# 512 weight columns to a bank per token tile in three projections of a two-layer backbone

## The chip, the cores and the metric

The kernel runs on one core of one Trainium2 chip. The metric is the time of one execution in microseconds on the device. Before the change, three runs gave a median of 1530.77 us (1530.55 to 1533.98).

## The reference, cut to what matters

The reference is a backbone of two layers over 256 latent tokens and 256 context tokens with 2048 channels, all in float32. An even layer (neighbourhood attention beside an S5 state-space group, one output projection) is followed by an odd layer (grouped-query attention). The three projections that the change touches are these:

```
# layer 0, for x (256 tokens) and for the context (256 tokens)
y = concat([za * silu(g_a), zb * silu(g_b)], -1) @ w_out        # ev_w_out 2048 x 2048
x = layer_norm(DN_ALPHA * x + gt * y, ln_g, ln_b)
# layer 1: w_in = [q 2048 | k 512 | v 512 | g 2048] columns
q, k, v, g = split(h @ w_in);  q, k = rms_norm(q), rms_norm(k)  # od_w_in; k, v for all 512 tokens
o = attention(rope(q), [rope(k), kc], [v, vc])                  # 16 heads over 4 key/value heads
y = (o * silu(g)) @ w_out                                       # od_w_out 2048 x 2048, 256 tokens
out = layer_norm(DN_ALPHA * x + gt * y, ln_g, ln_b)
```

## The kernel before

All work is in tiles of 128 partitions. The activations lie transposed, 16 channel tiles by 512 tokens, as a high part `big_h` and a low part `big_l`, both in the rounded type fp32r. Columns 0 to 255 are the context and 256 to 511 are x, until the last attention writes its output for x into the first 256. A *half* is one of these, two token tiles of 128. A product is made of three matmuls (high by high, high by low, low by high).

The weights come in pieces of 1024 columns by 128 partitions (512 KB) through the class `Stream` (lines 338 to 419). A piece passes through a DMA on SyncE's queue into a `raw` buffer, through ScalarE, which rounds it into a `hi` buffer, and through VectorE, which subtracts the two into a `lo` buffer (called the low part here). `fill` (line 395) issues these three steps ahead of use: low parts up to as many pieces ahead as there are `lo` buffers, high parts up to the number of `hi` buffers. There are 4 raw, 4 hi and 3 lo buffers, one more hi and lo from the output projection of layer 0 on (line 1557), and 3 hi and 4 lo more in the last projection (line 1864). `get` calls `fill` and hands out one piece. Each engine runs its instructions in the order in which the program issues them.

In the three projections a piece is 4 channel tiles by 256 weight columns, and `bform` and `bpart` (lines 497 and 506) put a block of 256 columns for both token tiles into one PSUM bank: per piece 2 token tiles by 4 channel tiles by 3 matmuls of 256 columns, 24 in all, and 4 pieces to a block. Two banks (`mm`, line 265) are used in turn. Five further banks (`bb2`, line 1554) serve transposes and attention.

- Output projection of layer 0 (`layer0_half`, line 1578): 8 blocks for the context half, then 8 for the x half. The first two blocks are begun ahead of the attention part's last writes (lines 1545 to 1549). After each block VectorE multiplies by the gate, adds the scaled input and takes the statistics (lines 1593 to 1596); this is called the eviction. The gate row is loaded by a DMA on SyncE's queue (line 1570).
- Between this and the next stage the x half is normalised in the background (`norm_h1`, line 1599), and tables for the rotary positions are made on VectorE from two small rows `grows` that come by DMA (lines 1658 to 1668).
- Keys and values (lines 1718 to 1730): for each half 2 blocks of keys and 2 of values. A block of keys goes through `k_done` (line 1695): ScalarE copies and squares, VectorE sums, GpSimd makes the inverse root, VectorE scales, TensorE transposes.
- Queries, gates and attention (lines 1800 to 1819) are not touched, but they share the banks.
- Output projection of layer 1 (lines 1820 to 1897): 2 blocks begun beside the last attention pair, 4 more, and a last part that does the last two blocks for the first token tile, then for the second, so that the first tile can be normalised while the second is still multiplied.

Background work (generators) is put between matmuls by `pump`, by due times that a model of the engines inside the program gives (class `Clock`). The model prices a 512-column matmul at 0.2162 and a 256-column one at 0.1082 (line 227).

Of the kernel before, what the change touches and what calls it, by code (L numbers as in the profile page):

```python
# [30 lines left out]
P = 128  # L31
D = 2048
# [216 lines left out]
def backbone(ctx: ExitStack, tc: tile.TileContext, A, out):  # L249
# [15 lines left out]
    mm = pool(ctx, name="mm", bufs=2, space=bass.MemoryType.PSUM)  # L265
# [26 lines left out]
    def mbank():  # L292
        return mm.tile([P, 512], F32, name="m")
# [44 lines left out]
    class Stream:  # L338
# [181 lines left out]

    def bform4(done):
# [60 lines left out]
    for half in range(2):  # L582
        for n in range(0, 8, 2):
            for n_, ko in ((0, 1), (1, 1), (0, 0), (1, 0)) if n == 0 and half == 0 else ((0, 1), (0, 0), (1, 1), (1, 0)):
                ws.add(W_OUT, D, ko * 8, 8, (n + n_) * 256, 256)
    for half in range(2):
        for n in range(4):
            for ko in (0, 1):
                ws.add(X_IN, OD_IN, ko * 8, 8, 2048 + n * 256, 256)
# [5 lines left out]
    NX = 2  # L595
    for n, a in ([(n, a) for n in range(NX) for a in range(3)] + [(n, 3) for n in range(NX)]
                 + [(n, a) for n in range(NX, 8) for a in range(4)]):
        ws.add(X_OUT, D, a * 4, 4, n * 256, 256)
# [946 lines left out]
    ps0 = [mbank().rearrange("p (t n) -> p t n", t=2) for _ in range(2)]  # L1545
    for i in range(4):
        if i == 1:
            zab = background(za_split())
        bpart(ps0[i // 2], 0, OUT_ORDER, i % 2)
# [4 lines left out]
    bb = pool(ctx, name="bb2", bufs=5, space=bass.MemoryType.PSUM)  # L1554
# [23 lines left out]
    def layer0_half(hf):  # L1578
# [3 lines left out]
        st_ = tp.tile([P, 2, 8, 6], F32, name="st0", bufs=2)  # L1582
        for n in range(8):
            cs = slice(n * 256, n * 256 + 256)
            xp = op.tile([P, 2, 256], F32, name="xp", bufs=2)
            GP.dma_start(xp, dram(src, n * 256, [[D, P], [P * D, 2], [1, 256]]))
            if hf == 0 and n < 2:
                ps = ps0[n]
                for a in (2, 3):
                    bpart(ps, 0, OUT_ORDER, a)  # L1590
            else:
                ps = bform(hf * T, OUT_ORDER)
            V.tensor_mul(t[:, :, cs], ps, gate[:, v, None, cs].to_broadcast([P, 2, 256]))
            V.scalar_tensor_tensor(t[:, :, cs], xp, ALPHA, t[:, :, cs], op0=OP.mult, op1=OP.add)
            for i in range(2):
                V.bn_stats(st_[:, i, n], t[:, i, cs])
# [75 lines left out]
    def rms(ps4):  # L1672

        sq = w1.tile([P, 2, 2, P], F32, name="sq", bufs=1).rearrange("p a b d -> p (a b) d")
        act(sq, ps4, AF.Square)
        ss = w1.tile([P, 4], F32, name="ss")
        V.tensor_reduce(ss, sq, axis=AX.X, op=OP.add)
# [17 lines left out]
    def k_done(hf, n, ps):  # L1695
        kn = w1.tile([P, 4, P], F32, name="kn")
        act(kn, ps.rearrange("p t (h d) -> p (t h) d", h=2))
        r = rms(kn)
        yield
        V.tensor_mul(kn, kn, r[:, :, None].to_broadcast([P, 4, P]))  # L1700
        kf = w1.tile([P, 2, 2, P], F32, name="kf")
        if hf == 0:
            V.tensor_mul(kf.rearrange("p t h d -> p (t h) d"), kn, grows[:, 1, None, :].to_broadcast([P, 4, P]))
        else:
            rope(kf, kn.rearrange("p (t h) d -> p t h d", t=2), 1)
        yield
        p = bank()
        for h in range(2):
            for t_ in range(2):
                PE.transpose(p[:, h * T + t_ * P:h * T + (t_ + 1) * P], kf[:, t_, h], ident)  # L1710
        o = slice(hf * T, hf * T + T)
# [248 lines left out]
```

## Time and profile before

| | |
|---|---|
| median of three runs | 1530.77 us |
| the profiled execution, its own time | 1534.4 us |
| its span, first to last instruction | 1532.5 us |
| TensorE matmuls (PE) busy | 1478.4 us, 96% |
| VectorE (DVE), ScalarE (ACT), GpSimd (POOL) busy | 982.8, 641.7, 154.1 us |
| mean granted TensorE clock | 0.986 |
| chain that ended last | PE 79%, DVE 7%, DMA 7%, issue 4% |

PE is busy in nearly every slice of the span, but a busy PE also holds what each matmul costs beside its columns. The chain is followed back from the last instruction to what released it at each step. The output projection of layer 0 lies between about 867 and 1073 us of the span, keys and values up to 1166 us, the attention stage up to 1441 us and the last projection up to 1517 us.

### The profile page before, as it was taken

How to read it: one execution, taken by the hardware profiler on the slowest of the kernel's cores; microseconds unless marked ns; L12 is line 12 of the kernel's file. 1: busy time of each engine (PE TensorE's matmuls, PEld its weight loads, DVE VectorE, ACT ScalarE, POOL GpSimd, SP SyncE). 2: the span in 40 equal slices, each digit the busy share in tenths (PEclk: the TensorE clock that was granted, in tenths of full speed). 3: DMA queues.
4: the chain of work that ended last, by engine and by line, in shares of the span. 5: the costliest groups of instructions: out<-in, count | busy, mean ns of one | idle time of the engine just before them, and what ended most of it. 6: DMA issues, size and time to landing. Idle time of an engine off the chain costs nothing.

```text
span 1532.5 us, 30530 instructions
## 1 busy us (share of the span) xinstructions
PE 1478.4 (96%) x12530; PEld 1283.4 (84%) x12530; DVE 982.8 (64%) x1721; ACT 641.7 (42%) x981; POOL 154.1 (10%) x308
## 2 busy tenths in 40 slices
PE   6998988999999999999999999999999999999996
PEld 3676777667789977888878999999899999999995
DVE  5356479988622688554447765665666666677597
ACT  2332244422355443433335533443454565665540
POOL 1000000000000033300000000100421211121021
PEclk8999999999999999999999999999999999999998
DMA  9998374676889577658877698886465445444684
GB/s 326 335 330 265 119 220 144 208 248 203 261 286 298 166 201 166 162 192 239 251 215 230 199 348 297 285 300 200 147 223 178 133 149 151 125 124 152 205 259 142
DMA packets 329919, 332.70 MB, mean 217 GB/s; under 512 B 40196, under 2 KB 287924, under 8 KB 329140
## 3 DMA queue, kind: packets, MB, share of 16 engines
q1 hardware_dynamic: 323540, 314.87, 65.8%
q0 software_dynamic: 6240, 15.88, 3.9%
q8 instruction: 98, 1.61, 0.4%
q14 instruction: 41, 0.34, 0.1%
HBM read 301.92 MB, written 24.54 MB: 213 GB/s over the span
## 4 chain that ended last, share of the span: by engine, by line
PE 79%; DVE 7%; DMA 7%; issue 4%; POOL 2%; SPq 1%; ACT 1%; DVEq 0%; POOLq 0%; ACTq 0%
PE m L212 59%; PE b L212 11%; PE a L212 6%; PE sb L212 4%; DVE dd L212 2%; DMA aw<-in_ada_w_dram 2%; DMA raw<-in_ev_w_in_dram 1%; DVE t L212 1%; SPq L212 1%; DVE lo L212 1%; DMA nat<-in_s_c_im_dram 1%; DMA gf<-in_ln_b_dram 1%; POOL gbr L212 1%; POOL rt L212 1%; DMA nat<-in_s_c_re_dram 1%
## 5 line engine op out<-in xcount | busy, mean ns | idle before, releaser
L212 ACT ACTIVATE hi<-raw 128x1024 fp32r<-128x1024 f32 (+1 forms) x253 | 265.2, 1050 | 319.2 <-PE m L212 166.5
L212 PE MATMUL m<-hi,big_h 128*128 128x256 f32 x1224 | 351.8, 287 | 0.1
L212 PE MATMUL m<-hi,big_l 128*128 128x256 f32 x1224 | 347.3, 284 | 0.0
L212 DVE TENSOR_TENSOR lo<-raw,hi 128x1024 fp32r<-128x1024 f32 (+1 forms) x214 | 257.2, 1209 | 110.9 <-issue 55.4
L212 PE MATMUL m<-lo,big_h 128*128 128x256 f32 x1152 | 326.9, 284 | 0.0
L212 PE MATMUL m<-big_h,hi 128*128 128x512 f32 (+1 forms) x848 | 319.6, 377 | 2.1 <-DVE acc L212 1.4
L212 PE MATMUL m<-big_l,hi 128*128 128x512 f32 (+1 forms) x848 | 309.3, 365 | 0.0
L212 PE MATMUL m<-big_h,lo 128*128 128x512 f32 (+1 forms) x832 | 304.6, 366 | 0.0
L212 PEld LDWEIGHTS m<-hi,big_h 128*128 128x128 f32 x1224 | 235.6, 192 | 7.3 <-issue 6.6
L212 PEld LDWEIGHTS m<-hi,big_l 128*128 128x128 f32 x1224 | 235.6, 193 | 0.2 <-DVE big_l L212 0.2
L212 PEld LDWEIGHTS m<-lo,big_h 128*128 128x128 f32 x1152 | 222.0, 193 | 0.1
L212 PEld LDWEIGHTS m<-big_h,hi 128*128 128x128 f32 x848 | 160.2, 189 | 39.9 <-issue 11.7
L212 PEld LDWEIGHTS m<-big_h,lo 128*128 128x128 f32 x832 | 157.1, 189 | 26.4
L212 PEld LDWEIGHTS m<-big_l,hi 128*128 128x128 f32 x848 | 160.5, 189 | 21.2
L212 PE MATMUL m<-lox,big_h 128*128 128x256 f32 x384 | 108.6, 283 | 0.0
L212 PE MATMUL m<-hix,big_h 128*128 128x256 f32 x312 | 89.1, 285 | 0.0
L212 PE MATMUL m<-hix,big_l 128*128 128x256 f32 x312 | 88.3, 283 | 0.0
L212 POOL DMA_DIRECT2D Yd<-ys x64 | 38.0, 600 | 407.7 <-DVE ys L212 407.0
L212 PEld LDWEIGHTS m<-lox,big_h 128*128 128x128 f32 x384 | 73.6, 192 | 0.3
L212 ACT ACTIVATE hix<-raw 128x1024 fp32r<-128x1024 f32 x45 | 47.5, 1056 | 49.9 <-PE m L212 16.9
L212 PE MATMUL a<-aw,cst 128*32 128x256 f32 x1024 | 65.4, 384 | 2.5 <-DMA aw<-in_ada_w_dram 2.4
L212 DVE TENSOR_TENSOR lox<-raw,hi 128x1024 fp32r<-128x1024 f32 x39 | 47.6, 1221 | 21.6 <-PE m L212 14.6
(383 smaller groups left out, 2192.9 us busy)
## 6 DMA issues: line engine op xcount, KB each, us to landing
aw<-in_ada_w_dram SPq DMA_DIRECT2D x128, 512.0 KB, 5.8
raw<-in_od_w_in_dram SPq DMA_DIRECT2D x96, 512.0 KB, 3.8
raw<-in_ev_w_in_dram SPq DMA_DIRECT2D x90, 512.0 KB, 5.0
adp<-in_ada_w_dram SPq DMA_DIRECT2D x64, 512.0 KB, 8.6
raw<-in_ev_w_out_dram SPq DMA_DIRECT2D x64, 512.0 KB, 6.1
raw<-in_od_w_out_dram SPq DMA_DIRECT2D x32, 512.0 KB, 4.9
ub<-Ud SPq DMA_DIRECT2D x32, 128.0 KB, 5.1
Sd<-sx SPq DMA_DIRECT2D x16, 256.0 KB, 6.5
```

The costliest lines, as they stand in the source:

```text
L212: r = f(*a, **kw)
```

## The change

In the three projections a piece becomes 2 channel tiles by 512 weight columns, and a PSUM bank holds 512 columns of one token tile. `wide` replaces `bform` there: a block of 512 columns takes two banks, one for each token tile, and 8 pieces, two at a time. With two pieces at hand it does both for the first token tile, then both for the second (24 matmuls of 512 columns in all). With the last two pieces (`a == 6`) no low parts are issued ahead before the first tile's bank is evicted (`done(0)`); then the low parts of two pieces (`ws.fill(2)`), then the second tile's matmuls and its eviction. The low and high parts of the next block's later pieces are issued as before, up to the number of buffers ahead, each time two pieces are taken.

The two `mm` banks become a ring of two single banks, to which a third is added from the output projection of layer 0 on; `bb2` has 4 banks in place of 5. The eviction is done for one token tile and 512 columns where it was two token tiles and 256. Keys: one token tile and four heads, where it was two token tiles and two heads. The last projection: three blocks of 512 columns (the first begun beside the last attention pair with 6 of its 8 pieces), and a last part of 512 columns for the first token tile and twice 256 for the second.

```diff
-    mm = pool(ctx, name="mm", bufs=2, space=bass.MemoryType.PSUM)
+    mm = pool(ctx, name="mm", bufs=1, space=bass.MemoryType.PSUM)
+    mring = [(mm, "m0"), (mm, "m1")]
...
-        def fill(self):
+        def fill(self, m=99):
...
-            nh, ns = min(self.i + self.n["hi"], n), min(self.i + self.n["lo"], n)
+            nh, ns = min(self.i + min(m, self.n["hi"]), n), min(self.i + min(m, self.n["lo"]), n)
...
+        def get2(self, fill=True):
+
+            if fill or self.ns < min(self.i + 2, len(self.jobs)):
+                self.fill()
+            self.i += 2
+            return self.tl.pop(self.i - 2), self.tl.pop(self.i - 1)
...
+    def wpart(ps, w, c, korder, a):
+
+        wh, wl = w
+        for k in range(2):
+            kk = korder[a * 2 + k]
+            PE.matmul(ps, big_h[:, kk, c:c + P], wh[:, k, :], start=a == 0 and k == 0, stop=False)
+            PE.matmul(ps, big_h[:, kk, c:c + P], wl[:, k, :], start=False, stop=False)
+            PE.matmul(ps, big_l[:, kk, c:c + P], wh[:, k, :], start=False, stop=a == 7 and k == 1)
+        pump()
+
+    def wide(t0, done, korder=tuple(range(KT)), ps=None, a0=0):
+
+
+        ps = ps or [mbank(), mbank()]
+        for a in range(a0, 8, 2):
+            w = ws.get2(a < 6)
+            for t in range(2):
+                for j in range(2):
+                    wpart(ps[t], w[j], t0 + t * P, korder, a + j)
+                if a == 6:
+                    done(t, ps[t])
+                    if t == 0:
+                        ws.fill(2)
...
-    bb = pool(ctx, name="bb2", bufs=5, space=bass.MemoryType.PSUM)
+    bb = pool(ctx, name="bb2", bufs=4, space=bass.MemoryType.PSUM)
+    mring.insert(0, (pool(ctx, name="mm2", bufs=1, space=bass.MemoryType.PSUM), "m2"))
...
-        for n in range(8):
-            cs = slice(n * 256, n * 256 + 256)
...
+        for n in range(4):
+            cs = slice(n * 512, n * 512 + 512)
...
+            def done(i, ps):
+                V.tensor_mul(t[:, i, cs], ps, gate[:, v, cs])
+                V.scalar_tensor_tensor(t[:, i, cs], xp[:, i], ALPHA, t[:, i, cs], op0=OP.mult, op1=OP.add)
+                V.bn_stats(st_[:, i, n], t[:, i, cs])
+
+            if hf == 0 and n == 0:
+                wide(0, done, OUT_ORDER, ps0, 4)
             else:
-                ps = bform(hf * T, OUT_ORDER)
...
+                wide(hf * T, done, OUT_ORDER)
...
+        def keys(t, ps):
+            kb_.append(background(k_done(hf, t, ps)))
+            pump()
+
+        def values(t, ps):
+            act(vh[:, 2 * hf + t], ps)
+            V.tensor_sub(vl[:, 2 * hf + t], ps, vh[:, 2 * hf + t])
+
+        wide(hf * T, keys)
+        wide(hf * T, values)
...
+        for n in range(3):
+            if n > 0:
+                wide(0, lambda i, ps: columns(n, i, ps), ps=[bank(), bank()])
+            else:
+                for i in range(2):
+                    columns(0, i, t[:, i, :512])
+            for c in (2 * n + 2, 2 * n + 3):
+                load_h1(c)
```

## Rows read from the trace of the kernel before

**Rows 1.** The page: TensorE's busy time, and its granted clock in 40 slices.
```profile
PE 1478.4 (96%) x12530; PEld 1283.4 (84%) x12530; DVE 982.8 (64%) x1721; ACT 641.7 (42%) x981; POOL 154.1 (10%) x308
...
PEclk8999999999999999999999999999999999999998
```

**Rows 2.** Windows of the three stages: start:end, length, busy and count per engine, clock, DMA, GB/s.
```profile
850.00:1072.00 222.00, 221.60 (x1929) 209.72 (x1928) 139.35 (x178) 89.20 (x101) 16.96 (x29) 1.00 0.81 275
1072.00:1166.00 94.00, 89.69 (x725) 88.79 (x725) 63.95 (x100) 43.98 (x57) 32.01 (x68) 0.96 0.57 182
1441.00:1517.00 76.00, 75.94 (x630) 75.50 (x630) 60.70 (x92) 24.60 (x25) 15.51 (x26) 1.00 0.80 240
```

**Rows 3.** Chain of waits, in order of time: start, length, what, matmuls.
```profile
778.58 12.96 PE m L212 x57
...
1166.44 36.00 PE m L212 x300
```

**Rows 4.** Timeline of VectorE around the last eviction of the x half.
```profile
1069.91 1.22 DVE L212 TENSOR_TENSOR lox<-raw,hi 128x1024 fp32r<-128x1024 f32 x1 [1.66 <-PE m L212]
1072.86 0.69 DVE L212 TENSOR_TENSOR t<-m,gate 128x512 f32<-128x512 f32 x1 [1.72 <-PE m L212]
1073.58 0.69 DVE L212 SCALAR_TENSOR_TENSOR t<-xp,t 128x512 f32<-128x512 f32 x1
1074.31 0.75 DVE L212 BATCH_NORM_STATS2 st<-t 128x6 f32<-128x256 f32 x2
1078.43 0.49 DVE L212 TENSOR_TENSOR rc<-tabs,grows 128x128 f32<-128x128 f32 x2 [3.37 <-DMA grows<-in_q_norm_g_dram]
...
1080.05 1.22 DVE L212 TENSOR_TENSOR lo<-raw,hix 128x1024 fp32r<-128x1024 f32 x1
```

**Rows 5.** Timeline of TensorE there: block's last matmul, next one, a later piece.
```profile
1072.54 0.28 PE L212 MATMUL m<-hi,big_l 128*128 128x256 f32 x1
1072.66 0.28 PE L212 MATMUL m<-hi,big_h 128*128 128x256 f32 x1
...
1078.54 0.28 PE L212 MATMUL m<-lox,big_h 128*128 128x256 f32 x1
```

**Rows 6.** Timeline of TensorE: first matmul of the output projection of layer 0.
```profile
866.84 0.28 PE L212 MATMUL m<-hi,big_h 128*128 128x256 f32 x1
```

**Rows 7.** Timeline of VectorE: the first eviction of that projection.
```profile
888.51 0.69 DVE L212 TENSOR_TENSOR t<-m,gate 128x512 f32<-128x512 f32 x1 [4.38 <-DMA gate<-Ad]
```

**Rows 8.** Timeline of SyncE's queue: issues of the gate rows and of `grows`.
```profile
880.40 0.81 SPq L212 DMA_DIRECT2D gate<-Ad  x2
...
1073.58 0.34 SPq L212 DMA_DIRECT2D grows<-in_q_norm_g_dram  x1
```

**Rows 9.** Timeline of TensorE: the x half's first transposes.
```profile
1089.81 0.43 PE L212 MATMUL b<-ident,t 128*128 128x128 f32 x1 [2.59 <-DVE t L212]
1091.07 0.90 PE L212 MATMUL b<-ident,t 128*128 128x128 f32 x3 [0.83 <-DVE t L212]
```

**Rows 10.** Windows of 10 us, columns as in Rows 2.
```profile
1000.00:1010.00 10.00, 9.60 (x97) 8.23 (x96) 5.00 (x6) 3.19 (x5) 0.00 (x0) 1.00 0.88 293
...
1090.00:1100.00 10.00, 9.17 (x55) 8.93 (x55) 7.76 (x12) 3.14 (x5) 6.28 (x13) 0.66 0.39 121
```

**Rows 11.** Timeline of ScalarE: the first block of keys.
```profile
1085.85 0.58 ACT L212 ACTIVATE kn<-m 128x512 f32<-128x512 f32 x1
1086.47 0.63 ACT L212 ACTIVATE sq<-kn 128x512 f32<-128x512 f32 x1
```

**Rows 12.** Timeline of VectorE: the same block's sum, and what follows it.
```profile
1090.93 0.68 DVE L212 TENSOR_REDUCE ss<-sq 128x4 f32<-128x512 f32 x1
...
1092.13 1.23 DVE L212 TENSOR_TENSOR lo<-raw,hi 128x1024 fp32r<-128x1024 f32 x1
```

**Rows 13.** Timeline of VectorE near the end: first eviction of the second tile.
```profile
1517.17 0.41 DVE L212 TENSOR_TENSOR t<-m,gate 128x256 f32<-128x256 f32 x1
```

**Rows 14.** Timeline of GpSimd near the end: last column loads and the last-norm rows.
```profile
1500.13 0.71 POOL L212 DMA_DIRECT2D xp<-Nd  x1 [7.50 <-DVE t L212]
...
1502.44 0.53 POOL L212 DMA_DIRECT2D gf<-in_ln_b_dram  x1
```

More of the change, by code (lines that the diff above doesn't have):

```diff
@@ L582, in backbone @@
     for half in range(2):
-        for n in range(0, 8, 2):
-            for n_, ko in ((0, 1), (1, 1), (0, 0), (1, 0)) if n == 0 and half == 0 else ((0, 1), (0, 0), (1, 1), (1, 0)):
-                ws.add(W_OUT, D, ko * 8, 8, (n + n_) * 256, 256)
+        for n in range(4):
+            for ko in (1, 0):
+                ws.add(W_OUT, D, ko * 8, 8, n * 512, 512)
     for half in range(2):
-        for n in range(4):
-            for ko in (0, 1):
-                ws.add(X_IN, OD_IN, ko * 8, 8, 2048 + n * 256, 256)
+        for n in range(2):
+            ws.add(X_IN, OD_IN, 0, KT, 2048 + n * 512, 512)
     for hp in range(8):
@@ L594, in backbone @@
             ws.add(X_IN, OD_IN, 0, KT, 3072 + (2 * hp + hh) * P, P)
[L595 to L598, printed above, removed]
+    NX = 6
+    for n in range(4):
+        ws.add(X_OUT, D, 0, KT, n * 512, 512)
     Ud = dr.tile([1024, 512], F32, name="Ud")
@@ L1544, in backbone @@
     OUT_ORDER = tuple(range(8, 16)) + tuple(range(8))
-    ps0 = [mbank().rearrange("p (t n) -> p t n", t=2) for _ in range(2)]
+    ps0 = [mbank(), mbank()]
     for i in range(4):
@@ L1548, in backbone @@
             zab = background(za_split())
-        bpart(ps0[i // 2], 0, OUT_ORDER, i % 2)
+        w = ws.get()
+        for t in range(2):
+            wpart(ps0[t], w, t * P, OUT_ORDER, i)
     force(zab)
@@ L1850, in backbone @@
         NH = 2
-        for n in range(NH - 1):
-            load_h1(n)
+        load_h1(0)
+        load_h1(1)
         def h1(n):
@@ L1859, in h1, with columns @@
             return xp
-        for n in range(NX):
-            bpart(first_ps[n], 0, range(KT), 3)
-            act(t[:, :, n * 256:n * 256 + 256], first_ps[n])
+        def columns(n, i, ps):
+            if i == 0:
+                inputs(n)
+            cs = slice(n * 512, n * 512 + 512)
+            V.tensor_mul(t[:, i, cs], ps, gate1[:, cs])
+            for c in range(2):
+                o = t[:, i, n * 512 + c * 256:n * 512 + c * 256 + 256]
+                V.scalar_tensor_tensor(o, xps[2 * n + c][:, i], ALPHA, o, op0=OP.mult, op1=OP.add)
+            V.bn_stats(st_[:, i, n], t[:, i, cs])
@@ L1864, in backbone, with inputs @@
+        xps = {}
+        def inputs(n):
+            for c in (2 * n, 2 * n + 1):
+                xps[c] = h1(c)
+        wide(0, lambda i, ps: act(t[:, i, :512], ps), range(KT), first_ps, NX)
         ws.more(wpool3, hi=3, lo=4)
         ws.fill()
[L1866 to L1874 removed]
@@ L1898, in backbone @@
-            V.bn_aggr(mv[:, i], st_[:, i])
+            for c in range(1 + i):
+                w = slice(256 * c, 256 * c + 512 - 256 * i)
+                ps = mbank()[:, w]
+                for a in range(8):
+                    if i == 0:
+                        pieces.append(ws.get())
+                    for k in range(2):
+                        wh, wl = (x[:, k, w] for x in pieces[a])
+                        xh, xl = (x[:, 2 * a + k, i * P:(i + 1) * P] for x in (big_h, big_l))
+                        PE.matmul(ps, xh, wh, start=a == 0 and k == 0, stop=False)
+                        PE.matmul(ps, xh, wl, start=False, stop=False)
+                        PE.matmul(ps, xl, wh, start=False, stop=a == 7 and k == 1)
+                if i == 0:
+                    columns(3, i, ps)
+                else:
+                    o = t[:, i, 1536 + 256 * c:1536 + 256 * c + 256]
+                    V.tensor_mul(o, ps, gate1[:, 1536 + 256 * c:1536 + 256 * c + 256])
+                    V.scalar_tensor_tensor(o, xps[6 + c][:, i], ALPHA, o, op0=OP.mult, op1=OP.add)
+                    V.bn_stats(st_[:, i, 3 + c], o)
```

108 lines of the change are left out of this document (36 added, 72 removed).

## The prediction

> **What bounds the kernel now.** I read the page first: TensorE is busy for 1478.4 of 1532.5 us, at full granted clock nearly throughout [rows 1]. Then the windows of the three stages that are changed: TensorE is busy for 221.6 of 222, 89.7 of 94 and 75.9 of 76 us, while VectorE has 37%, 32% and 20% to spare [rows 2]. So in these stages time is the number of matmuls times their spacing, plus the few stalls of the middle stage. The third view, the chain of waits, gives the spacing: 300 matmuls of 256 columns run end to end in 36.00 us, 0.1200 us each; 57 of 512 columns, in the projections that already use them, in 12.96 us, 0.2274 us each [rows 3]. Both at clock 1.00. Twice 0.1200 is 0.2400: two narrow ones cost 12.6 ns more than one wide one. Feeding TensorE is not the limit: the low part made at 1069.91 is ready at 1071.13 [rows 4] and first used at 1078.54 [rows 5], 7.4 us early.
>
> **The change, part by part.**
>
> *Matmuls.* The output projection of layer 0 has 2 halves x 8 blocks x 4 pieces x 24 = 1536 narrow matmuls; they become 768 wide ones. Keys and values: 2 x 4 x 96 = 768 become 384. The last projection: 768, of which 96 stay narrow (the second tile's last part) and 672 become 336. That is 1488 wide ones. At 12.6 ns: 9.7 + 4.8 + 4.2 = 18.7 us less. All of it lies on the path. The shape is measured, but with the weights as the stationary operand; here the activations are. Bounds: 0 (if this other arrangement kept twice 0.1200) and 1488 x 0.0267 = 39.7 (if a wide one cost only 512 columns at 2.4 GHz, 0.2133). I take 18.7, since size and type of both operands are those of the row.
>
> One rule speaks against it. The Trainium skill (TensorE: Matmul & The Clock Gate, "Wait — 56ns, not 53.3ns?") puts the fixed cost of a warm matmul at some 2.5 ns beside its columns over 2.4 GHz. The trace differs: 0.1200 is 13.3 ns above 256 columns, 0.2274 is 14.1 ns above 512 [rows 3]. By the page's 2.5 ns the gain would be an estimated 3.7 us; by the rows it is 18.7, and the measurement decides.
>
> *Order at a block's end.* The new wait. Today three low parts stand ready when a block ends. After the change `get2` issues none with the last two pieces; the next block's first two are issued behind the first tile's eviction, on VectorE, and the next block's second matmul waits for the first of them. Let B be the end of the first tile. VectorE starts 0.20 us after the last matmul's successor begins (1072.66 to 1072.86) [rows 4, 5], then 0.72 for the product, 0.73 for the sum, some 0.7 for statistics, 1.22 for the low part [rows 4]: ready at B + 3.57. TensorE meanwhile has the second tile's 12 matmuls, 2.73 us, and one more of 0.23 that needs the high part only: B + 2.96. It stalls for 0.6 us, at 8 blocks less the first: 7 x 0.6 = 4.2 us. Bounds: 0, and 7 x 2.6 = 18 if another background instruction of 2 us stood ahead each time. I add 1.0 for background work that does so in the x half.
>
> *The first block.* Its eviction already waits 4.38 us for the gate row and starts at 888.51 [rows 7]; that DMA was issued at 880.40 [rows 8], behind the attention's last writes, which don't move. TensorE starts the projection at 866.84 [rows 6] and ends the first tile after 48 + 24 + 12 matmuls, 19.1 us on, at 885.9; it wants the next low part at 888.9. That is ready at 888.51 + 0.72 + 0.73 + 0.7 + 1.22 = 891.9. A stall of 3.0 us that the three ready low parts cover today. Bounds: 0.6 (gate early) and 5.5 (with a fall of the clock, priced below).
>
> *Between the projection and keys.* E is the end of the x half (B + 2.73). VectorE: eviction to E - 0.4, two low parts (2.4) to E + 2.0, the second tile's product to E + 2.7. Today `grows` is issued at 1073.58, the moment that product ends, and VectorE resumes 4.85 us later at 1078.43; the table work ends at 1080.05 [rows 4, 8]. So: tables from E + 7.6 to E + 9.2, the third low part at E + 10.4. TensorE has two pieces only: it starts 0.6 late, runs 24 x 0.2274 = 5.5, and one more of 0.2: it stops at E + 6.3 for 4.1 us. What is late next: the x half's transposes, which today stall for 2.59 and 0.83 us [rows 9], 3.4 together. With TensorE held up before them they find their data, and I count them as gone. The clock: after today's stalls it is 0.66 in a window with 55 matmuls where 83 would fit [rows 10]; 28 x 0.12, less the 0.83, is 2.5 us lost. I take the same after. Net + 0.7. Bounds: -6 (all of today's stall and slow clock gone, none new) and +7.5 (both kept).
>
> *Keys.* At B ScalarE copies and squares (some 0.6 each) [rows 11], VectorE sums (0.7) and goes on to small operations until the low part, 1092.13 - 1090.93 = 1.2 in all [rows 12]; with 0.2 at the start that is B + 2.6, and the low part at B + 3.8 to 4.0. A stall of 1.0 us, twice: 2.0. Bounds 0 and 6 (3 each, GpSimd's chain ahead). Values: copy 0.6, subtraction 0.7, low part 1.22, with 0.2 some 2.7, inside 2.96: nothing.
>
> *Last projection.* 8 low buffers instead of 4: the next block's first four low parts are issued before its predecessor's last two pieces. No stall. The tail: today VectorE comes to the second tile's first eviction at 1517.17 [rows 13], after the first tile's normalisation, hardly after TensorE's end; the column loads that feed it were issued at 1500.13 and 1502.44 [rows 14], behind the block before. Both move with the block. I count 0, with -1 and +3 as bounds.
>
> *Banks.* A wide block's first bank is always the third, idle one; the second was evicted 5 us before. Four banks for attention: in a pair of heads a bank comes round to work that has to wait for its reader anyway. 0, at most 8 pairs x 0.83 (the nearest stall on a bank's work [rows 9]) = 6.6. Pieces stay at 512 KB; runs of 2 KB instead of 1 KB in memory can only help a DMA share of 0.81 [rows 2], covered by TensorE: 0. Eviction work is the same number of elements.
>
> **Sum:** -18.7 + 4.2 + 1.0 + 3.0 + 0.7 + 2.0 = -7.8 us. On the profiled execution's own 1534.4 us (2 us around its span) that is 1526.6. That execution is 3.6 above the median of the runs; on 1530.8 it is 1523.0.
>
> **Rivals.**
>
> 1. *The stalls don't come.* The planner puts work elsewhere, or VectorE gets the low parts out in time; only the first block and the tables remain. Then -18.7 + 3.0 + 0.7 = -15.0: 1515.8. For it: VectorE's spare time [rows 2]. Against: order in the queue, not spare time, makes the low part late.
> 2. *The margin is gone everywhere.* A piece is held for two thirds of a pair, and low parts are only some 4 us early in mid-block where they were 7.4. Background work of keys and of normalisation then stalls TensorE within blocks too, doubling the 10.9 us of costs: -18.7 + 21.8 = +3: 1534; nothing or little is won, 1527 to 1535.
> 3. *Slower: block ends take the clock along.* At each of the 12 block ends in the first two stages the stall could be followed by a clock of 1.2 GHz, as at 1090 [rows 10], 2.5 us each. It decides from six such ends: 10.9 + 15 exceeds the gain by 7. With ten: +17, 1548. For it: a stall of 2.6 and 0.8 us did so. Against: a stall of 0.4 us at 1004 left the clock at 1.00 [rows 10].
> 4. *The wide matmul gains nothing with the activations stationary.* Then the costs stand alone, +10.9: 1541.7. Against: rows 3. By the skill's 2.5 ns above it would be an estimated 1538.
>
> **How the numbers follow.** My forecast 0.50 (own range 1518 to 1528), the first rival 0.20, the second 0.17, the third 0.09, the fourth 0.04. A measurement of this kernel tells 0.3%, 4.6 us, from no change: faster is below 1526.2, slower above 1535.4. Faster: most of the forecast (0.43) and the first rival, 0.63. No change: 0.07 of the forecast, 0.14 of the second rival, 0.01 of the others: 0.22. Slower: 0.15. The range of 8 in 10 reaches from full success, 1512, into the second rival, 1533.
>
> **What would show it.** Wide matmuls 0.227 us apart in the chain of waits; any other spacing breaks the first term. A gap of some 0.6 us in TensorE at block ends of the first projection, put down to a low part; one of 3 us near 889 behind the gate row; one of 4 us some 6 us into the keys, behind the tables, and none at the x half's transposes. No gap in the last projection or attention. If TensorE shows no gap at block ends, the order of low parts was misread; if the gaps exceed 18 us together, the forecast is wrong in sign.

## The result, and the profile after

The changed kernel takes 1547.01 us (median of four runs, 1541.99 to 1551.86) beside 1530.66 for the kernel before on the same chip (four runs, 1527.84 to 1533.98): ratio 1.0101, interval 1.0069 to 1.0133. It is slower by 16 us, where 8 us less were predicted. The profiled execution took 1551.86, 4.9 above its median, with a span of 1550.1.

The page of the changed kernel; the first line answers to [rows 1].

```profile
PE 1469.8 (95%) x11042; PEld 1206.4 (78%) x11042; DVE 978.6 (63%) x1699; ACT 641.6 (41%) x981; POOL 148.9 (10%) x300
...
PEclk9999999999999999999999999999899999999997
```

TensorE issues 1488 matmuls fewer, as the change says, and is busy for 8.6 us less; the span is 17.6 us longer. So TensorE is waiting. Windows of the three stages in the changed kernel, columns as in [rows 2]:

```profile
868.00:1078.00 210.00, 201.90 (x1090) 156.47 (x1089) 123.00 (x149) 81.79 (x92) 10.96 (x21) 0.98 0.76 268
1078.00:1190.00 112.00, 98.68 (x438) 79.41 (x437) 71.14 (x103) 47.47 (x63) 32.99 (x68) 0.95 0.53 171
1428.00:1534.00 106.00, 98.70 (x494) 83.45 (x492) 74.57 (x112) 40.14 (x51) 15.46 (x26) 0.97 0.64 207
```

The windows of [rows 2] and the ends of stages given with them don't fit these: counted matmul by matmul, keys and values end at 1177.8 us before the change and not at 1166, and the last projection begins at 1416.6 and not at 1441. The same stages before, in windows that fit:

```profile
867.00:1073.00 206.00, 205.60 (x1860) 196.57 (x1859) 128.07 (x166) 82.56 (x93) 16.96 (x29) 1.00 0.82 279
1073.00:1178.00 105.00, 100.69 (x817) 99.79 (x816) 70.67 (x106) 49.06 (x64) 32.01 (x68) 0.97 0.58 182
1417.00:1517.00 100.00, 99.94 (x821) 98.96 (x821) 75.32 (x115) 39.52 (x50) 15.51 (x26) 1.00 0.72 218
```

Before, TensorE had no idle time to speak of in the first and the last stage and 4 us in the middle one; after the change it has 8, 13 and 7 us, and the clock is under 1 in all three. Who is waited for, by TensorE in these stages of the changed kernel (total, times, longest):

```profile
PE m L212 <- DVE lox L212: 9.8, 2, 5.8
PE b L212 <- DVE kf L212: 7.1, 3, 3.5
PE m L212 <- DVE lo L212: 6.1, 8, 2.4
PE a L212 <- DMA aw<-in_ada_w_dram: 3.8, 5, 1.8
PE b L212 <- DVE lox L212: 1.5, 1, 1.5
```

The same view of the kernel before:

```profile
PE b L212 <- DVE t L212: 3.4, 2, 2.6
PE b L212 <- DVE kf L212: 0.9, 2, 0.7
PE a L212 <- DMA aw<-in_ada_w_dram: 0.4, 1, 0.4
```

With 0.2 us for `t` these are 28.5 us of waits in place of 4.7. `lo` and `lox` are low parts, `kf` the normalised keys ahead of their transposes, `aw` the weights of a background product (the modulation of layer 1) whose matmuls are spread over the first projection. On top, TensorE's records show half clock (1.2 GHz) for 24 us of these stages, in five stretches; before it was one, of 6.8 us. Of the time in which TensorE works at half clock, half is lost: without the parts that fall into stops this is 9.3 us in place of 3.0.

The table gives my reading of all traces: us from a stage's first matmul to the next stage's first, and from TensorE's last matmul to the end of the span. Attention took 238.8 us in every one. Each row is one profiled execution, while the ratio rests on four to ten runs of each kernel. The change, w_only and keys_v have the same code in the first projection (both halves), and their traces show 209.9, 203.6 and 204.4 us there; so a difference of a few us in one stage counts only where several rows or the ratio bear it out.

| kernel | context half | x half | keys, values 0 | keys, values 1 | last projection | behind it | ratio to before |
|---|---|---|---|---|---|---|---|
| before | 98.4 | 107.4 | 56.8 | 48.3 | 100.8 | 15.2 | 1 |
| the change | 101.5 | 108.4 | 64.5 | 46.9 | 105.8 | 15.8 | 1.0101 |
| w_only | 98.5 | 105.1 | 57.0 | 48.4 | 100.5 | 17.5 | 0.9999 |
| kv_only | 98.4 | 107.5 | 52.8 | 46.9 | 100.5 | 16.9 | 0.9967 |
| xo_only | 98.4 | 108.1 | 55.1 | 48.4 | 106.8 | 14.1 | 1.0053 |
| fill_first | 98.7 | 106.5 | 51.5 | 45.4 | 109.1 | 16.7 | 1.0016 |
| wkv_fill | 99.9 | 106.1 | 51.5 | 45.4 | 100.5 | 16.5 | 0.9955 |
| xo_raw6 | 98.4 | 107.7 | 53.9 | 48.4 | 103.4 | 14.8 | 1.0004 |
| xo_nh4 | 98.4 | 107.3 | 55.0 | 48.5 | 112.2 | 14.1 | 1.0059 |
| all_fill_raw6 | 97.9 | 104.9 | 51.5 | 45.4 | 102.6 | 17.8 | 0.9959 |
| keys_v | 98.9 | 105.5 | 63.3 | 49.2 | 106.6 | 15.3 | 1.0068 |
| wkv_fill_aw | 100.5 | 100.5 | 51.3 | 45.4 | 101.0 | 21.0 | 1.0080 |
| xo_raw6_fill | 98.4 | 108.5 | 55.4 | 48.4 | 99.6 | 18.6 | 0.9996 |
| all_late | 101.2 | 100.5 | 49.2 | 45.8 | 100.4 | 19.8 | 1.0079 |
| wkv_aw_late | 100.4 | 100.5 | 51.3 | 45.4 | 100.5 | 17.5 | 0.9926 |
| wkv_aw_late_gr | 100.0 | 100.5 | 49.3 | 45.4 | 100.5 | 16.1 | **0.9915** |
| after_aw_late | 105.1 | 108.4 | 64.1 | 47.5 | 106.5 | 14.1 | 1.0124 |
| all_late2 | 99.7 | 100.5 | 49.3 | 45.4 | 100.3 | 17.1 | 0.9937 |

### The profile page after: what moved, and what is told of

It reads as the page before. It is cut to its first block, busy times and chain, and to the rows that moved or that the text cites. A ratio compares the mean times of both kernels' runs of the same rounds, so it can differ in the third digit from the quotient of the medians.

```text
span 1550.1 us, 27508 instructions
## 1 busy us (share of the span) xinstructions
PE 1469.8 (95%) x11042; PEld 1206.4 (78%) x11042; DVE 978.6 (63%) x1699; ACT 641.6 (41%) x981; POOL 148.9 (10%) x300
## 4 chain that ended last, share of the span: by engine, by line
PE 73%; DMA 9%; DVE 9%; issue 5%; POOL 2%; SPq 1%; ACT 1%; DVEq 0%; POOLq 0%; ACTq 0%
PE m L212 54%; PE b L212 10%; PE a L212 5%; PE sb L212 3%; DVE dd L212 2%; DMA aw<-in_ada_w_dram 2%; DMA raw<-in_ev_w_in_dram 2%; DVE t L212 2%; SPq L212 1%; DVE lo L212 1%; POOL rt L212 1%; DMA nat<-in_s_b_im_dram 1%; DMA tt<-kp 1%; DMA nat<-in_s_c_im_dram 1%; DMA gate<-Ad 1%
## 5 line engine op out<-in xcount | busy, mean ns | idle before, releaser
L212 PE MATMUL m<-hi,big_h 128*128 128x256 f32 (+1 forms) x816 | 274.7, 337 | 0.0
L212 PE MATMUL m<-hi,big_l 128*128 128x256 f32 (+1 forms) x816 | 269.6, 330 | 0.0
L212 PE MATMUL m<-lo,big_h 128*128 128x256 f32 (+1 forms) x782 | 258.7, 331 | 6.1 <-DVE lo L212 6.1
L212 PEld LDWEIGHTS m<-hi,big_h 128*128 128x128 f32 x816 | 156.2, 191 | 20.3 <-issue 6.4
L212 PEld LDWEIGHTS m<-hi,big_l 128*128 128x128 f32 x816 | 156.3, 192 | 14.1
L212 PEld LDWEIGHTS m<-lo,big_h 128*128 128x128 f32 x782 | 149.9, 192 | 21.7 <-DVE lo L212 9.5
L212 PE MATMUL m<-lox,big_h 128*128 128x512 f32 (+1 forms) x194 | 68.1, 351 | 9.9 <-DVE lox L212 9.8
L212 PE MATMUL m<-hix,big_h 128*128 128x512 f32 (+1 forms) x160 | 56.3, 352 | 0.0
L212 PE MATMUL m<-hix,big_l 128*128 128x512 f32 (+1 forms) x160 | 55.4, 346 | 0.0
L212 PEld LDWEIGHTS a<-aw,cst 128*32 128x32 f32 x1024 | 27.9, 109 | 34.6 <-issue 10.2
```

The costliest lines, as they stand in the source:

```text
L212: r = f(*a, **kw)
```

## The experiments

### Which of the three projections loses

Each alone in the form of the change, the other two as before; the helpers and the banks are those of the change in all. The last two lines are an edit of the whole change: low parts are issued with the last pair as well, ahead of the first tile's eviction.

```diff
 w_only:   +  ws.add(W_OUT, D, ko * 8, 8, n * 512, 512)
 kv_only:  +  ws.add(X_IN, OD_IN, 0, KT, 2048 + n * 512, 512)
 xo_only:  +  ws.add(X_OUT, D, 0, KT, n * 512, 512)
 fill_first:
-            w = ws.get2(a < 6)
+            w = ws.get2()
```

> Only the output projection of layer 0 takes the new form; keys, values and the last projection keep 256-column blocks of two token tiles, in the same ring of three banks and with four banks for attention. Theory A (each stage loses by its own waits: low parts, transposes and ada weights come late behind longer groups on VectorE and SyncE's queue): this stage took 4.1 us longer in the trace after (205.8 to 210.0), so +4, about 1535, with gaps near 891 (gate row), of 0.4 at block ends, and ada matmuls that wait for their weights; the 4 us stop behind the tables stays, since the block before it is wide. Rival B (the loss is in what the stages share, the ring of banks and the fall of the clock from run to run): this alone is already near 1545.

Measured: 0.9999 (0.9980 to 1.0018): no loss, where theory A expected 4 us and the rival more.

> Only keys and values take the new form. Theory A: the stage took 6.3 us longer in the trace after, of which the stop behind the tables (4.0) belongs to the block before it, which is narrow here and leaves three low parts; what is left is the transposes of the keys that wait for GpSimd's two inverse roots in a row (7.1 us of gaps) against a gain of 4.8: +1 to +4, 1532 to 1535. Rival B: near 1545.

Measured: 0.9967 (0.9951 to 0.9983), a gain where a loss was expected.

> Only the last projection takes the new form. Theory A: the stage took 5.0 us longer in the trace after, by gaps of 1.5 and 5.8 us and a slow clock behind the second, as VectorE does two tiles' evictions and four scaled inputs in one go and the raw buffers stay full meanwhile: +5, 1535 to 1537. Rival B: near 1545. Third theory C (the last projection only suffers because it comes late in DMA traffic that the others shift): no gap over 2 us here, and a gain of 4, 1527.

Measured: 1.0053 (1.0031 to 1.0075), with two stops, of 1.66 and 5.84 us, in the last projection.

> The whole change, but with the last two pieces of a block low parts are issued ahead too, so that the next block's first two stand before the first tile's eviction on VectorE. Theory A: the gaps of 0.4 at seven block ends (3), of 0.9 at two ends of keys (1.7) and of 2.4 near 891 go, and the stop behind the tables shrinks from 4.0 to about 2, as the second tile's product no longer waits for two low parts: 9 us less than the change, about 1538; the keys' transposes and the last projection's gaps stay. Rival D (the eviction, not the low part, is what TensorE would then wait for, because the bank comes round): no gain, about 1547, with gaps in front of a tile's first matmul.

Measured: 1.0016 (0.9998 to 1.0033). The one argument gives back 13 of the 16 us. The stalls of 0.42 us at block ends are gone, the 4 us in front of the tables are 1.6 and the wait for `kf` is 1.2 instead of 7.1; the last projection is no better (109.1 us, with a stop of 6.12). What it does to the first block, on VectorE of fill_first (compare the row at 890.62 further down):

```profile
887.87 1.22 DVE L212 TENSOR_TENSOR lo<-raw,hi 128x1024 fp32r<-128x1024 f32 x1 [4.17 <-ACT hi L212]
889.01 0.68 DVE L212 TENSOR_TENSOR t<-m,gate 128x512 f32<-128x512 f32 x1
```

The low part comes first, and the gate's row is no longer waited for with low parts queued behind it.

So two things are told apart. The last projection loses by itself. The other two gain or are even when alone, and lose together (10.4 us in the trace of the change): the three alone add up to +0.2%, all at once are +1.0%.

### The last projection

VectorE in the last projection of the changed kernel, around the end of a block:

```profile
1481.05 0.68 DVE L212 TENSOR_TENSOR xp<-xp,gbr 128x512 f32<-128x512 f32 x1
1482.81 0.69 DVE L212 TENSOR_TENSOR xp<-xp,gbr 128x512 f32<-128x512 f32 x1 [1.08 <-DMA gbr<-in_ln_b_dram]
1485.23 0.69 DVE L212 TENSOR_TENSOR xp<-xp,gbr 128x512 f32<-128x512 f32 x1 [1.73 <-DMA gbr<-in_ln_g_dram]
1486.75 0.69 DVE L212 TENSOR_TENSOR xp<-xp,gbr 128x512 f32<-128x512 f32 x1 [0.82 <-DMA gbr<-in_ln_b_dram]
1487.36 0.68 DVE L212 TENSOR_TENSOR t<-b,gate 128x512 f32<-128x512 f32 x1
...
1490.98 0.69 DVE L212 BATCH_NORM_STATS2 st<-t 128x6 f32<-128x512 f32 x1
1491.59 1.21 DVE L212 TENSOR_TENSOR lox<-raw,hix 128x1024 fp32r<-128x1024 f32 x1
...
1500.97 1.23 DVE L212 TENSOR_TENSOR lo<-raw,hi 128x1024 fp32r<-128x1024 f32 x1 [4.76 <-ACT hi L212]
```

For 10.5 us, 3.6 of them waiting for the columns' scale and offset (`gbr`), there is no low part. The four raw buffers stay full, so no load is issued from 1481.2 to 1492.8; then four low parts in a row, and VectorE is idle for 4.76 us because ScalarE is, which waits for the loads:

```profile
1499.88 1.06 ACT L212 ACTIVATE hi<-raw 128x1024 fp32r<-128x1024 f32 x1 [8.75 <-DMA raw<-in_od_w_out_dram]
```

Three edits on xo_only: more raw buffers; the column loads two blocks ahead, which takes the waits out of the group; and low parts between the two tiles' evictions beside the raw buffers.

```diff
 xo_raw6, xo_raw6_fill:
-        ws.more(wpool3, hi=3, lo=4)
+        ws.more(wpool3, raw=2, hi=3, lo=4)
 xo_nh4:
-        NH = 2
+        NH = 4
...
-            for c in (2 * n + 2, 2 * n + 3):
+            for c in range(2 * n + 4, min(2 * n + 6, 8)):
 xo_raw6_fill, behind the statistics in columns():
+            if i == 0 and n < 3:
+                ws.fill(6)
```

> Only the last projection wide, with 6 raw buffers there in place of 4; nothing else differs from xo_only. Theory F (VectorE's group of four scaled inputs and two evictions, 10.5 us of it in xo_only, holds all four raw buffers; afterwards four low parts run and VectorE idles 4.6 us until the next transfers land): with two buffers more six low parts follow the group, the gaps of 1.7 and 5.8 us and the slow clock behind them go: stage about 97 us instead of 106.8, ratio 0.996 to 0.998. Rival G (VectorE has simply too much work there): no change, 1.005. Rival H (the scaled inputs' own transfers, 3.4 us of waits in the group): less than half of it goes.

Measured: 1.0004 (0.9988 to 1.0019); stops of 2.54 and 2.90 us instead of 1.66 and 5.84, the stage 3.4 us shorter where theory F expected 10. It gains, so rival G (too much work for VectorE, no change) is out, but more than half of the stops is left, as rival H had it; the next run speaks against H.

> Only the last projection wide, 4 raw buffers, but the scaled inputs are loaded two blocks ahead (4 buffers each instead of 2), so that VectorE doesn't wait for them inside the group. Theory F: the group shrinks from 10.5 to 7 us, the cycle of eight low parts and a group from about 24.6 to 21 us, just under the 21.8 us in which TensorE uses eight pieces: gaps shrink to 0 to 3 us, ratio 0.998 to 1.002. Rival H: all gaps go, 0.997. Rival G: no change.

Measured: 1.0059 (1.0033 to 1.0085). The group of VectorE shrinks from 10.5 to 6.9 us and the stops stay (11.5 us in all, beside 7.5 in xo_only). Theories F and H expected a gain; neither has it. Rival G's "no change" came true here, after xo_raw6 had spoken against it. The rows of VectorE behind that group in xo_nh4:

```profile
1488.60 1.23 DVE L212 TENSOR_TENSOR lo<-raw,hi 128x1024 fp32r<-128x1024 f32 x1 [5.11 <-ACT hi L212]
1493.65 1.23 DVE L212 TENSOR_TENSOR lo<-raw,hi 128x1024 fp32r<-128x1024 f32 x1 [3.83 <-ACT hi L212]
```

The time saved in the group is waited for again: with four raw buffers what limits is the turn of a raw buffer (loaded, high part, low part, free), not VectorE's work.

> Only the last projection wide, with six more raw buffers' worth of room as in the run with raw=2 more (six in all), and six of the next block's low parts issued on VectorE between the first tile's eviction and the second's. Theory F (VectorE is the bound of the stage because it does the group of 10 us without a low part in between, and the raw buffers stand full meanwhile): the gaps of 2.5 and 2.9 us shrink to under 2 us in all, the last stage goes from 103.4 to 100.5 to 101.5 us, the ratio from 1.0004 to 0.997 to 0.999. Rival T (the transfers' arrival is what the low parts wait for): VectorE then waits in order for high parts with the second tile's eviction queued behind them, the idle time only moves to this place, and the stage stays at 103 us or grows, ratio 1.000 to 1.004.

Measured: 0.9996 (0.9978 to 1.0015); the last projection 99.6 us, 1 below the kernel before and 4 below xo_raw6, with stops of 1.25 and 1.37 us. Raw buffers and the order of low parts together take the stops from 7.5 to 2.9 us, so these are their cause; the order alone was not tried. But the time does not fall as expected, for 18.6 us follow TensorE's last matmul in place of 15.2: VectorE is at the first tile's normalisation until 1513.9, 3.3 us past TensorE's end, and then evicts the second tile. What TensorE saves here, VectorE's tail takes back.

### Everything, or all but the last projection

wkv_fill is fill_first with the last projection narrow; all_fill_raw6 is fill_first with six raw buffers in the wide one.

```diff
 wkv_fill:       -  ws.add(X_OUT, D, 0, KT, n * 512, 512)
 all_fill_raw6:  +  ws.more(wpool3, raw=2, hi=3, lo=4)
```

> The output projection of layer 0, keys and values wide, low parts issued ahead with the last two pieces too; the last projection narrow as before. In fill_first the first two stages took 205.1 and 96.9 us where before took 205.8 and 105.1, and the last 109.1 where before took 100.8. Theory A (the stages' losses add up, and only the last projection is left as a loss): 0.7 + 8.3 = 9 us less than before, ratio 0.994. Rival (a gain here comes back in the last projection, as the pieces arrive in another state): no better than 0.999.

Measured: 0.9955 (0.9934 to 0.9976), as expected, and the lowest so far; of the others only kv_only's interval lies below 1.

> The whole change with low parts ahead at block ends and 6 raw buffers in the last projection. Theories A and F together: 9 us less in the first two stages and 3 to 4 less in the last: 12 us less than before, ratio 0.992. If F is wrong, as fill_first: 1.002.

Measured: 0.9959 (0.9936 to 0.9981), less than expected; one stop of 4.94 us is left in the last projection.

### The keys' chain on GpSimd

In the changed kernel both tiles' keys are ready 2.7 us apart. GpSimd is busy with small operations from 1107.39 to 1118.82, the first tile's inverse root and then the second's, and TensorE, which has the transposes in its queue, waits:

```profile
1108.42 0.50 PE L212 MATMUL m<-lo,big_h 128*128 128x512 f32 x1 [0.85 <-DVE lo L212]
1116.58 1.02 PE L212 MATMUL b<-ident,kf 128*128 128x128 f32 x4 [3.51 <-DVE kf L212]
```

```diff
-        r = rms(kn.rearrange("p (a b) d -> p a b d", a=2))
+        r = rms(kn.rearrange("p (a b) d -> p a b d", a=2), V)
```

> The changed kernel, with the keys' inverse root of the mean square on VectorE and no longer on GpSimd; nothing else differs. Theory G (the two tiles' chains queue one after the other on GpSimd, and the transposes that TensorE has queued wait for them): the waits of TensorE for kf in the profile, 7.1 us in the change (3.5 + 2.7 + 0.9), fall below 1.5 us in all, the first half of the keys and values goes from 64.5 us to 55 to 59, and the ratio to the kernel before goes from 1.0101 to about 1.005. Rival N (the normalisation of the x half, which is late because of the tables' wait, holds VectorE, and GpSimd's chain is beside the point): kf waits stay above 4 us and the ratio stays at 1.008 to 1.012.

Measured: 1.0068 (1.0042 to 1.0095). The wait for `kf` falls from 7.1 to 2.1 us, so shortening the chain on GpSimd takes most of it away; the stage gains only 1.2 us, and the two ratios' intervals overlap. The chain is now on VectorE, ahead of the low parts:

```profile
1105.54 0.50 PE L212 MATMUL m<-lo,big_h 128*128 128x512 f32 x1 [2.63 <-DVE lo L212]
1114.34 0.66 PE L212 MATMUL b<-ident,kf 128*128 128x128 f32 x4 [2.15 <-DVE kf L212]
```

The stop at the block's end has grown from 0.85 to 2.63, and again in the other half. Theory G has the wait right and misses the stage's time by 4 us or more. The chain is not the whole reason, though. fill_first leaves it on GpSimd, where it is as long (1093.4 to 1104.9), and waits 1.2 us; kv_only waits 1.5. What differs is the place of the transposes in TensorE's order: in the change both tiles' stand behind the 114th matmul of this half, in fill_first behind the 132nd and 144th, in kv_only behind the 138th and 150th, four to eight us later. The program's planner puts them there, and by its prices (line 240: 0.10 us for such an operation on GpSimd, 0.15 more until its result is read) twelve in a row take 3.0 us where one tile's took 6.7. That a better price would remove the wait was not tried.

### The weights of the background product

SyncE's queue in wkv_fill, issues of loads; from the first row to the second none is issued for 10.5 us, and the `aw` load of the third stands behind the raw load of the second:

```profile
996.23 0.33 SPq L212 DMA_DIRECT2D aw<-in_ada_w_dram  x1
1007.10 0.38 SPq L212 DMA_DIRECT2D raw<-in_ev_w_out_dram  x1
1007.58 0.41 SPq L212 DMA_DIRECT2D aw<-in_ada_w_dram  x1
```

Whom this queue waits for from 990 to 1010 us (total, times, longest): a low part, which frees a raw buffer.

```profile
SPq L212 <- DVE lox L212: 10.5, 1, 10.5
```

Of TensorE's waits for `aw`, one of 1.85 us at 1018 comes behind this pause. The one of 3.29 us at 997 comes ahead of it, behind a like pause of the queue from 987.4 to 992.7.

The first edit moves all of layer 1's loads of this kind to GpSimd's queue, the second only the quad that is loaded in these stages (`s == 2`). The last diff loads the keys' gain rows early.

```diff
 wkv_fill_aw, all_late:
-                SY.dma_start(tiles[n], ...)
+                (GP if l == 1 else SY).dma_start(tiles[n], ...)
 wkv_aw_late, wkv_aw_late_gr, after_aw_late, all_late2:
+                (GP if l == 1 and s == 2 else SY).dma_start(tiles[n], ...)
 all_late, wkv_aw_late_gr, all_late2, ahead of layer0_half(0):
+    grows = const.tile([P, 2, P], F32, name="grows")
+        GP.dma_start(grows[:, i], dram(A[nm], 0, [[0, P], [1, P]]))
```

> The version with both wide projections ahead of attention, the fill ahead of each pair, and the narrow last projection (0.9955 of the kernel before), with the ada weights of layer 1 loaded on GpSimd's DMA queue and no longer on SyncE's. Theory Q (these loads stand on SyncE's queue behind weight loads that wait for their buffers): TensorE's waits for aw, 5.5 us there, fall below 1.5 us, its clock doesn't fall at 1010 to 1020, and the ratio goes to 0.991 to 0.993. Rival B (the transfers are late because the 16 DMA engines are full, whatever queue they stand on): aw waits stay at 3 to 6 us and the ratio at 0.994 to 0.997; GpSimd's own loads of the h input could then be later too.

Measured: 1.0080 (1.0053 to 1.0107), and yet the x half takes 100.5 us instead of 106.1 and the wait for `aw` is gone. The loss is ahead of the changed stages, where the first projection now starts 21 us later (890.8). GpSimd's waits from 500 to 790 us in wkv_fill_aw:

```profile
POOL aw L212 <- PE a L212: 166.1, 8, 64.9
POOL Yd L212 <- DVE ys L212: 66.6, 12, 17.5
```

A load that waits for its buffer holds the stores (`Yd`) behind it, now on this queue, as in these two rows of GpSimd:

```profile
542.47 0.58 POOL L212 DMA_DIRECT2D aw<-in_ada_w_dram  x1 [10.76 <-PE a L212]
543.05 2.40 POOL L212 DMA_DIRECT2D Yd<-ys  x4
```

That is the first part of the loss: matmul for matmul, TensorE goes from 13 us ahead of wkv_fill to 19 behind between 506 and 570 us of wkv_fill. By 652 us it is only 4 behind, and then falls back to 21 where no store is left on the queue; there VectorE waits for the rows of the neighbourhood attention's bias, which come on SyncE's queue (3.8 us of such waits in wkv_fill):

```profile
DVE bias L212 <- DMA bias<-Rd: 26.4, 4, 11.2
```

They are issued beside bursts of up to eight `aw` loads on GpSimd's queue. Both readings come from the trace alone.

> The whole change with the fill ahead of each pair, six raw buffers in the last projection (0.9959 so far), and three edits more: six low parts between the two tiles' evictions in the last projection, the ada weights of layer 1 on GpSimd's queue, and the keys' and queries' gain rows loaded ahead of the first wide projection into a tile of their own. If the theories of SyncE's queue (5 us of stalls and the clock behind them), of the gain rows (1.7 us and the clock) and of the last projection (5 us) all hold: 0.986 to 0.990. If the last projection's stalls are a matter of transfers: 0.990 to 0.993. If none of the three does anything: 0.996.

Measured: 1.0079 (1.0046 to 1.0112), with the same loss ahead of the changed stages (the first projection starts at 897.1); the first half of its keys and values takes 49.2 us.

> Both wide projections ahead of attention, the fill ahead of each pair and the narrow last projection (0.9955 of the kernel before), with only the last quad of ada weights (layer 1, the gate, loaded during the first wide projection) on GpSimd's DMA queue. Theory Q (on SyncE's queue these loads stand behind weight loads that wait for their buffers): TensorE's waits for aw, 5.5 us there, under 1 us; the x half from 106.1 to 100.5 to 102 us; no loss ahead of the first wide projection; ratio 0.991 to 0.993. Rival B (the 16 DMA engines are full there, whatever the queue): aw waits 3 us or more, x half over 104 us, ratio 0.994 to 0.997.

Measured: 0.9926 (0.9908 to 0.9944). TensorE in the x half, wkv_fill and then wkv_aw_late:

```profile
969.00:1076.00 107.00, 101.52 (x582) 79.88 (x581) 66.90 (x86) 42.32 (x51) 6.81 (x15) 1.00 0.72 247
```

```profile
965.00:1066.00 101.00, 100.79 (x579) 79.89 (x579) 66.87 (x86) 42.09 (x50) 15.02 (x29) 1.00 0.78 267
```

The same work, without the 5.5 us. It was the queue and not the DMA engines behind it: their share rises from 0.72 to 0.78. This agrees with a sentence of the Trainium skill (DMA: Bandwidth & Descriptors, "Anatomy of one DMA — SWDGE (gpsimd) path") by which a DMA's wait is done by the sequencer that issues it.

> As the run above, and the rows of the keys' and queries' gains loaded on GpSimd's queue ahead of the first wide projection, into a tile that waits for nobody, so that VectorE's tables don't wait for them at the start of the keys. If the 1.7 us gap there is that wait: it goes, the first half of keys and values goes from 51.3 to about 49.3 us, ratio 0.001 below the run above (0.990 to 0.992). If the gap is the low parts' own turnaround: no difference to the run above.

Measured: 0.9915 (0.9890 to 0.9940), the fastest version: 1516.90 us beside 1530.26. The 1.74 us in front of the tables are gone and that stage goes from 51.3 to 49.3 us; the two ratios' intervals overlap, so the step is shown by the trace alone. From the first projection to the span's end TensorE's clock stays at 1.00 until its last matmuls are done, and these waits are left:

```profile
PE m L212 <- DVE lox L212: 2.1, 3, 0.9
PE m L212 <- DVE lo L212: 1.4, 3, 0.8
PE b L212 <- DVE kf L212: 0.9, 1, 0.9
PE b L212 <- DVE t L212: 0.2, 1, 0.2
```

> The changed kernel with the last quad of ada weights on GpSimd's queue and nothing else altered. Theory Q: the 3.8 us of aw waits go and with them the half-clock stretch at 1015; the x half goes from 108.4 to 102 to 104 us, ratio from 1.0101 to 1.005 to 1.007. Rival B: aw waits stay over 2 us, the x half at 107 us or more, ratio 1.009 to 1.011.

Measured: 1.0124 (1.0094 to 1.0154): no gain, where 0.4% was expected. VectorE at the first block, the changed kernel and then after_aw_late:

```profile
890.62 0.69 DVE L212 TENSOR_TENSOR t<-m,gate 128x512 f32<-128x512 f32 x1 [3.76 <-DMA gate<-Ad]
```

```profile
896.38 0.69 DVE L212 TENSOR_TENSOR t<-m,gate 128x512 f32<-128x512 f32 x1 [5.35 <-DMA gate<-Ad]
```

The gate's row is there 14.6 us after its issue on SyncE's queue (881.76) where it took 11.2 (879.41); whether the moved loads delay it was not tried. Since VectorE waits for it ahead of the low parts, TensorE stops for 4.20 us instead of 2.43; 1.8 us of `aw` waits stay, and a new stop of 2.55 us for a low part comes behind them. So in the changed kernel the move removes half of the 3.8 us only, and rival B has the x half (108.4 us) and the missing gain right. The same edit is worth 0.3% where low parts come first and nothing where they don't.

> The second run's version with the wide last projection as well (six raw buffers there and six low parts between its two tiles' evictions). The last stage of the run that had all layer-1 loads moved was 100.4 us beside 100.5 to 100.8 us narrow, with 19.8 us from TensorE's end to the span's beside 15 to 18. So theory V (VectorE bounds the end: what TensorE saves is waited for by tile 0's normalisation and the second tile's evictions) expects the same ratio as the second run within 0.002, or up to 0.003 worse. If the matmul saving of 4 us arrives at the end it is 0.002 to 0.003 better.

Measured: 0.9937 (0.9917 to 0.9957). The wide last projection gains nothing (100.3 us and 17.1 behind it, beside 100.5 and 16.1). Theory V has the number, but VectorE's tail, 1.0 us longer, is only a part of the reason: one stop of 2.58 us and 3.4 us at half clock behind it are left and use up most of the 4 us.

## Why the prediction was wrong

*Matmuls: right.* Spacing of the starts is 0.227 us in all three stages of the changed kernel, activations stationary, 0.120 for the narrow ones: the 18.7 us are there. By the 2.5 ns of the Trainium skill (TensorE: Matmul & The Clock Gate, "Wait — 56ns, not 53.3ns?") a wide matmul would take an estimated 0.216; the trace doesn't agree. The fourth rival is out: wkv_aw_late_gr gains 0.85% with 1152 of the 1488. The windows of [rows 2] don't fit the stages, as said above, but no term of the sum hangs on their ends.

*Stalls that were foreseen: right in size, and fewer.* Block ends 0.42 us (0.6 predicted) and at four of the seven ends only, the first block 2.43 (3.0), the tables 4.02 (4.1), keys' block ends 0.85 and 0.88 (1.0). TensorE's timeline in the changed kernel:

```profile
893.95 0.50 PE L212 MATMUL m<-lo,big_h 128*128 128x512 f32 x1 [2.43 <-DVE lo L212]
...
920.15 0.50 PE L212 MATMUL m<-lo,big_h 128*128 128x512 f32 x1 [0.42 <-DVE lo L212]
...
1088.85 0.50 PE L212 MATMUL m<-lox,big_h 128*128 128x512 f32 x1 [4.02 <-DVE lox L212]
```

*The failed steps.* First, the term of the last projection, "No stall": it has 7.3 us of stops. I counted low buffers, eight of them, and left out that they are filled through four raw buffers while VectorE does a group of 10.5 us. Second, the term of the keys: its two stalls on low parts came, but the keys' transposes wait 7.1 us, where it was 0.9 before. Two tiles' chains on GpSimd now come together behind a place in TensorE's order that the planner chose too early; the prediction had the chain in a bound and not in the sum. (The x half's transposes, "I count them as gone", do find their data.) Third, nothing was counted for the background product, whose loads stand on SyncE's queue behind raw loads; an order of low parts sets when raw buffers come free, and so when everything behind them on that queue is issued. TensorE waits 3.8 us for it in place of 0.4. Fourth, the clock: the price of one fall was kept as before, but four of the five larger stops in the first two stages and the largest of the last one bring their own. Windows of the changed kernel behind the stop of 2.43 us, behind one of 0.42, behind one of 1.84 (for `aw`) and in that of 5.77 (columns as in [rows 2]; the clock is the third figure from the end, 0.61, 1.00, 0.61, 0.61):

```profile
894.00:898.00 4.00, 4.00 (x11) 3.15 (x12) 3.93 (x5) 1.22 (x2) 0.72 (x1) 0.61 1.02 364
920.00:930.00 10.00, 9.85 (x66) 7.29 (x67) 7.84 (x9) 2.12 (x2) 0.71 (x1) 1.00 0.76 249
1018.00:1022.00 4.00, 4.00 (x12) 3.09 (x12) 0.84 (x1) 1.06 (x1) 0.00 (x0) 0.61 0.81 237
1512.00:1515.00 3.00, 0.00 (x0) 0.00 (x0) 2.93 (x5) 2.58 (x3) 1.71 (x3) 0.61 0.18 61
```

None is seen behind the stops of 0.42 us. By the spacing of the matmuls' starts, stops cost 33.0 us in place of 5.9 and half clock outside of them 8.8 in place of 2.6. Less 18.7 the stages come to +14.6 us; they measure +15.4, and 1.5 before them and 0.7 behind make the 17.6 of the span. The prediction's own sign, gaps of more than 18 us together, was met.

So no rival describes what happened. The second came nearest in kind (too little margin), but named stalls on low parts within blocks, and there are hardly any. The third has the number, 1548, by chance: it was made of block ends that take the clock along, and none of them with 0.42 us did. The order at a block's end was priced by the stall that shows there, 0.4 us. Its larger price is elsewhere: for the whole of a block's last pair `wide` issues no high part and no low part before the eviction. fill_first shows the price: one argument, 13 us. That the supply does not recover before the next disturbance is my reading of it, not measured by itself.

*Banks: right.* Attention took 238.8 us with four banks as with five.

*Open.* Why w_only and kv_only alone come off so much better than together is not settled. For the first projection it is in part the spread between executions, 203.6 to 209.9 us with the same code; for keys and values the traces show the stop in front of the tables (3.55 us in w_only too), the place of the transposes and the clock.

## What to carry to other kernels

Merging matmuls saves its 12.6 ns each only while the supply keeps up; when the supply is a chain of small buffers (load, high part, low part), the time between two issues of its work counts, not the number of finished pieces ahead. Put the supply's next step ahead of an eviction in an engine's order whenever the eviction can wait for something else, such as a row from memory. And when a stall is mended, look at the queue that its loads stand on before moving anything: the same move was worth 0.3%, nothing, or -1.2%, by what else stood there.

## What the runs showed of the hardware beside this

TensorE's clock fell within a stop or up to 1 us behind it, and the length of the single stop does not decide: in wkv_fill it fell behind stops of 0.92 and 0.76 us close together, and stayed at 1.00 behind one of 3.29 us.

```profile
896.00:899.00 3.00, 3.00 (x10) 2.35 (x9) 2.86 (x6) 1.06 (x1) 0.00 (x0) 0.58 1.04 417
1000.00:1004.00 4.00, 3.68 (x24) 2.83 (x25) 1.28 (x3) 2.37 (x4) 0.00 (x0) 1.00 0.21 83
```

That last stop was a wait for `aw`; behind shorter waits for the same loads the clock did fall (1.84 us in the change, 2.68 in fill_first). What decides was not tried. An inverse root of 128x4 elements took twelve operations and 6.7 us on GpSimd (1107.39 to 1114.1), some at 0.2 and some at 1.1 us for the same form; on VectorE, with steps fused, it is nine operations and 1.7 us (1102.60 to 1104.26 in keys_v). The kernel before, unchanged, gave 1524.5 to 1545.2 us in all but one of the runs beside these kernels, so ratios of 0.3% need runs side by side.
